# Two-layer decoder trunk: low parts of attention projection weights by accumulating transfers, top-k rounds spread between weight units

## The chip, the core and the metric

The kernel runs on one core of a Trainium2 chip. The metric is device time in microseconds (us) of one execution, the median of the runs shown. The engines are named as in the profile: PE (TensorE, matrix multiply), PEld (its weight loads), DVE (VectorE), ACT (ScalarE), POOL (GpSimd) and SP (SyncE, which here only issues transfers).

## What is computed

One sequence of 512 tokens, width 1024, two layers. Layer 0 is a gated recurrent block, layer 1 is attention over a chosen subset of keys; each is followed by a squared-ReLU MLP of width 4096. Everything is float32. The part that the change touches is the attention layer:

```python
def dsa_mixer(h, w_in, kv_norm_g, w_uk, w_uv, w_o, rel_bias):
    topk = min(TOPK_MAX, S // 4)                            # 128 of 512 keys
    q, c, qi, ki, wi = jnp.split(h @ w_in, ATT_IN_SPLITS, axis=-1)
    c = rms_norm(c, kv_norm_g)                              # latent keys/values, 128 wide
    q_lat = jnp.einsum('bshd,hdc->bshc', q, w_uk) * ATT_SCALE
    ...
    dots = jax.nn.relu(jnp.einsum('bqhd,bsd->bqhs', qi_b, ki))   # 8 index heads
    score = jnp.einsum('bqh,bqhs->bqs', wi_b, dots)              # causal
    _, idx = lax.top_k(score, topk)                              # per query
    logits = q_lat_b . c_sel + bias;  p = softmax(logits);  o = p . c_sel
    ...
    return o @ w_o
```

## The kernel before

**Three products for one.** Each float32 matrix product is made of three PE passes over rounded operands of type float32r. A weight tile `raw` is split into a high part `wh` (the rounded copy, made by ACT, line 268) and a low part `wl = raw - wh` (line 269); activations are split in the same way into `xh` and `xl`. `mm3` (lines 295 to 297) then runs wh with xh, wh with xl and wl with xh into one PSUM accumulator.

**Weight units.** All weights are cut into units of 128x1024 numbers (512 KB), eight blocks of 128x128 each, in the order in which they are used (`PLAN`, `SEQ`). One unit is 24 matmuls. `unit(u)` hands out a unit and prepares those up to five ahead (`LA = WH - 1`), so that loads (line 223, issued by SP), the cast on ACT and the subtraction on DVE or POOL run ahead of PE. There are six buffers for `wh` and six for `wl`, so the cast of a unit waits until PE is done with the unit six before it. `LO_POOL` names the 16 units whose low part POOL makes: of the indexer projections `a_idx` 0, 1, 2 and 4, all eight of the query projection `a_q`, the value matrix `uv`, and the first three of the output projection `w_o`. All others are made by DVE.

**The attention stage.** After the MLP of layer 0, five `a_idx` units give the index queries and keys; after the second of them the mean square of the tokens is taken (`att_st0`: PE line 377, then a chain of small DVE instructions on 128x4 numbers, lines 385 to 396, called with ACT's square root in `rsqrt_tok` and `diag`), and after the third it is broadcast to all partitions by two matmuls with ones (`bcast`, lines 413 and 414). `idx_head` then forms the scores of eight heads; some (head, row block) pairs are scaled and added by POOL (`SCORE_POOL`, lines 872 and 874), the others by DVE (line 876). One unit `a_c` gives the latent keys. The two `uk` units are split by ACT (line 246) and POOL (`ukl`, line 248).

**Top-k** finds the 128th largest score of each row by rounds of eight: the maxima (line 931) and their replacement (line 936), for two of the three row blocks in each round, all on DVE. `topk_steps` is a generator, and `pump(n)` issues n rounds; so the program text decides where rounds stand between other DVE work. Once a row block is done its mask is written (lines 941 and 942).

**The order.** `ATT_HEAD` is a list of steps written out by hand: `q` is one query unit (ev_q: scale on DVE, line 1018, then casts on ACT and subtractions on POOL, lines 880 to 883), `pN` is N top-k rounds, `M` is the mean of the latent keys (c_mean: the same chain of small DVE instructions as above), `F` its broadcast and the normalized keys (c_fin), `L` loads a bias, `k`, `A`, `v`, `n` are steps of single heads. Then `ATT_LOOP` runs the heads in a software pipeline. The framework places each engine's instructions in an order near that of the text, and each engine runs its own list in order.

Of the kernel before, what the change touches and what calls it, by code (L numbers as in the profile page):

```python
# [12 lines left out]
F32R = mybir.dt.float32r  # L13
BF16 = mybir.dt.bfloat16
AF = mybir.ActivationFunctionType
ALU = mybir.AluOpType
# [22 lines left out]

ATT_HEAD = ("q q M q F p1 p1 q L3 q L1 L2 p1 q p2 p2 L0 p2 p1 k0 k1 p2 p1 p1 q A1 A0 v00 v01 p1 v02 n0 k2 n1 v03 q "
            "p2 p1 p1000")

ATT_LOOP = "KAa0Bk1b2xyzeGnfgm"
V_ITER = 6
# [94 lines left out]
PLAN, SEQ = build_plan()  # L141
# [3 lines left out]
SRC = []  # L145
# [2 lines left out]
    SRC.append([MEM.setdefault(_k, len(MEM)) for _k in _keys])  # L148
NMEM = len(MEM)

LO_POOL = {PLAN[n][0] + i for n, w in (("a_idx", (0, 1, 2, 4)), ("a_q", range(8)), ("uv", (0,)), ("w_o", range(3))) for i in w}


@with_exitstack
def tile_trunk(ctx: ExitStack, tc: tile.TileContext, xT, wu, prm, bias, out):
    nc = tc.nc
# [10 lines left out]
    def bt(dt, name):  # L167
        cnt[0] += 1
        return big.tile([P, S], dt, tag="b", name=f"{name}_{cnt[0]}")
# [36 lines left out]
    prepped = {}  # L206
    state = {"next": 0}

    def lo_engine(u):
        return nc.gpsimd if u in LO_POOL else nc.vector  # L210

    UK0 = PLAN["uk"][0]

    def load_raw(u):
        res = []
        for i, n in enumerate(SRC[u]):
            raw = wraw.tile([P, 1024], F32, tag="raw", name=f"raw_{u}_{i}")
            if u == 0:
                nc.sync.dma_start(raw[:, :S], wu[n][:, :S])
                nc.sync.dma_start(x[0], xT[:, 0])  # L220
                nc.sync.dma_start(raw[:, S:], wu[n][:, S:])
            else:
                nc.sync.dma_start(raw, wu[n])
            res.append(raw)
        return res
# [11 lines left out]
    def prep(u):  # L237
        raws = pre_raw.pop(u) if u in pre_raw else load_raw(u)
        kind = SEQ[u][0]
        raw = raws[0] if raws else tsum.pop("P3")  # L240
        if UK0 <= u < UK0 + 2:
            h = []
            l = []
            for j in range(2):
                hh = bt(F32R, "ukh")
                nc.scalar.copy(hh, raw[:, j * S:(j + 1) * S])
                ll = bt(F32R, "ukl")
                nc.gpsimd.tensor_sub(ll, raw[:, j * S:(j + 1) * S], hh)
                h.append(hh)
                l.append(ll)  # L250
            prepped[u] = (h, l)
            return
        if kind == "#T1":
            raw = tsum["T1"] = raws[1]
            nc.vector.tensor_sub(raw, raw, raws[0])
        elif kind == "#T2":
            nc.vector.tensor_sub(raw, raw, tsum.pop("T1"))
            tsum["T2"] = raw
        elif kind == "#T4":
            nc.vector.tensor_sub(raw, raw, tsum.pop("T2"))  # L260
        elif kind == "#P7":
            tsum["P3"] = raw
            raw = raws[1]
            nc.vector.tensor_sub(raw, raws[0], raw)
        wh = whl.tile([P, 1024], F32R, tag="wh", name=f"wh_{u}")
        wl = whl.tile([P, 1024], F32R, tag="wl", name=f"wl_{u}")
        for c in ((slice(0, S), slice(S, 2 * S)) if u == 0 else (slice(0, 2 * S),)):
            nc.scalar.copy(wh[:, c], raw[:, c])  # L268
            lo_engine(u).tensor_sub(wl[:, c], raw[:, c], wh[:, c])  # L269
        prepped[u] = (wh, wl)  # L270
        if kind[:2] == "#P":
            prepped[u] += split_act(aq.pop((kind, SEQ[u][1][1])), "a")
# [580 lines left out]
    for t in (1, 2, 3):  # L853
        score[t] = bt(F32, "score")
        w = (t + 1) * P
# [102 lines left out]
    def pump(n):  # L958
        for _ in range(n):
            next(tk, None)  # L960
# [41 lines left out]
    pump(2)  # L1002
    for m, ps in Phase("a_c", nx2.xh, nx2.xl).step():
        ev_c(ps)
    pump(4)
    ukh = []
    ukl = []
    for g in range(2):
# [189 lines left out]

    for w in ATT_HEAD.split():
        if w[0] == "p":  # L1200
# [208 lines left out]
```

## Time and profile before

| | before |
|---|---|
| median of 3 runs | 1099.59 us (1098.83 to 1101.01) |
| the profiled execution, its own time | 1101.33 us |
| its span (first to last instruction) | 1099.5 us |
| busy: PE / DVE / ACT / POOL | 1072.0 / 763.9 / 619.5 / 166.2 us |
| share of the span: PE / DVE / ACT / POOL | 97% / 69% / 56% / 15% |
| granted TensorE clock, mean | 0.98 |
| chain that ended last: PE / DVE / ACT / POOL | 84% / 8% / 5% / 1% |

PE has work nearly all the time, so a change can shorten the run where PE stands idle or runs at a lower granted clock. In the page's 40 slices PE is below nine tenths only in three around the middle (the attention stage, from about 520 to 630 us) and in the last one. The shares are averages over the whole run: what an engine does in the attention stage is read from windows and timelines of that stage.

### The profile page before, as it was taken

What the parts mean: (1) busy time and instruction counts of PE and PEld (TensorE: products, weight loads), DVE (VectorE), ACT (ScalarE), POOL (GpSimd) and SP (SyncE); (2) the same over time, 40 slices, a digit from 0 to 9 for tenths busy, and PEclk for the clock granted to TensorE, in tenths of its full rate; (3) what the DMA queues carried; (4) which work ended last, traced back from release to release, by engine and by line L of the source; (5) the groups of instructions that cost most, each with busy time, mean ns of one, the idle gap of its engine ahead of it and who ended that gap; (6) DMA issues with size and microseconds to landing.
All of it is one profiled execution on the core that took longest, in us unless ns stands there. A gap on an engine that the chain in (4) does not pass through costs nothing.

```text
span 1099.5 us, 13547 instructions
## 1 busy us (share of the span) xinstructions
PE 1072.0 (97%) x4908; PEld 884.2 (80%) x4908; DVE 763.9 (69%) x1175; ACT 619.5 (56%) x1041; POOL 166.2 (15%) x203
## 2 busy tenths in 40 slices
PE   9999999999999999999798899999999999999996
PEld 7887888888888888888686688888888888888885
DVE  6579995555555559987799979845545555557995
ACT  7379754444444546756444789733644444546463
POOL 0000021000000000019387665312000000000000
PEclk9799999999999999999898899999999999999998
DMA  8222233444443445563313212023234444444562
GB/s 308 77 96 77 80 131 115 134 134 136 135 149 129 141 153 172 192 194 123 105 57 115 87 39 69 1 76 117 96 119 150 146 141 153 134 151 137 169 215 77
DMA packets 40532, 138.30 MB, mean 126 GB/s; under 512 B 4625, under 2 KB 4625, under 8 KB 40465
## 3 DMA queue, kind: packets, MB, share of 16 engines
q1 hardware_dynamic: 40032, 136.86, 38.0%
q8 instruction: 38, 0.62, 0.2%
q10 hardware_dynamic: 432, 0.58, 0.2%
q14 instruction: 30, 0.24, 0.1%
HBM read 135.32 MB, written 2.10 MB: 125 GB/s over the span
## 4 chain that ended last, share of the span: by engine, by line
PE 84%; DVE 8%; ACT 5%; issue 1%; POOL 1%; DMA 0%; DVEq 0%; ACTq 0%; POOLq 0%
PE mm L295 16%; PE mm L296 16%; PE mm L297 15%; PE sp L756 9%; PE sp L754 9%; PE sp L755 9%; PE o L1171 2%; DVE work L936 2%; DVE m L931 2%; PE tr L1146 1%; PE st L618 1%; PE qk L1099 1%; ACT wh L268 1%; PE qk L1100 1%; PE qk L1102 1%
## 5 line engine op out<-in xcount | busy, mean ns | idle before, releaser
L268 ACT CAST wh<-raw 128x1024 fp32r<-128x1024 f32 (+1 forms) x228 | 237.8, 1050 | 359.4 <-PE mm L296 206.0
L269 DVE TENSOR_TENSOR wl<-raw,wh 128x1024 fp32r<-128x1024 f32 (+1 forms) x212 | 259.1, 1226 | 210.7 <-ACT wh L268 210.1
L295 PE MATMUL mm<-xh,wh 128*128 128x512 f32 x752 | 295.8, 394 | 0.2 <-ACT xh L355 0.2
L296 PE MATMUL mm<-xl,wh 128*128 128x512 f32 x752 | 295.6, 393 | 0.0
L297 PE MATMUL mm<-xh,wl 128*128 128x512 f32 x752 | 295.3, 393 | 0.0
L296 PEld LDWEIGHTS mm<-xl,wh 128*128 128x128 f32 x752 | 142.8, 190 | 31.0 <-DVE xl L357 1.1
L295 PEld LDWEIGHTS mm<-xh,wh 128*128 128x128 f32 x752 | 143.1, 190 | 30.5 <-ACT xh L355 0.8
L297 PEld LDWEIGHTS mm<-xh,wl 128*128 128x128 f32 x752 | 142.7, 190 | 29.8
L754 PE MATMUL sp<-wh,ah 128*128 128x512 f32 x320 | 124.9, 391 | 0.0
L756 PE MATMUL sp<-wh,al 128*128 128x512 f32 x320 | 124.6, 389 | 0.0
L755 PE MATMUL sp<-wl,ah 128*128 128x512 f32 x320 | 124.5, 389 | 0.0
L269 POOL TENSOR_TENSOR wl<-raw,wh 128x1024 fp32r<-128x1024 f32 x16 | 39.6, 2478 | 332.5 <-ACT wh L268 325.9
L754 PEld LDWEIGHTS sp<-wh,ah 128*128 128x128 f32 x320 | 60.1, 188 | 12.7 <-ACT t L717 0.5
L756 PEld LDWEIGHTS sp<-wh,al 128*128 128x128 f32 x320 | 60.1, 188 | 12.6
L755 PEld LDWEIGHTS sp<-wl,ah 128*128 128x128 f32 x320 | 60.1, 188 | 12.3
L368 POOL TENSOR_TENSOR sq<-sq,sq 128x512 f32<-128x512 f32 x21 | 34.4, 1637 | 210.9 <-ACT sq L364 185.9
L234 DVE TENSOR_TENSOR al<-h,ah 128x512 fp32r<-128x512 f32 x80 | 55.4, 701 | 2.0 <-ACT ah L232 1.7
L754 PE MATMUL sp<-wh,sh 128*128 128x512 f32 x128 | 50.0, 391 | 0.0
L756 PE MATMUL sp<-wh,sl 128*128 128x512 f32 x128 | 49.9, 392 | 0.0
L755 PE MATMUL sp<-wl,sh 128*128 128x512 f32 x128 | 49.8, 389 | 0.0
L719 ACT ACTIVATE h<-t 128x256 f32<-128x256 f32 x128 | 46.5, 411 | 2.1
L232 ACT CAST ah<-h 128x512 fp32r<-128x512 f32 x80 | 46.7, 619 | 0.5
(258 smaller groups left out, 1645.8 us busy)
## 6 DMA issues: line engine op xcount, KB each, us to landing
raw<-in_wu_dram SPq DMA_DIRECT2D x244, 512.0 KB, 3.4
bias<-in_bias_dram SPq DMA_DIRECT2D x16, 256.0 KB, 3.0
x<-in_xT_dram SPq DMA_DIRECT2D x8, 256.0 KB, 6.4
out_dram<-out SPq DMA_DIRECT2D x6, 256.0 KB, 2.1
raw<-in_wu_dram SPq DMA_DIRECT2D x2, 256.0 KB, 3.7
gB<-in_prm_dram SPq DMA_DIRECT2D x2, 256.0 KB, 5.5
out_dram<-out ACTq DMA_DIRECT2D x2, 256.0 KB, 2.9
prm_sb<-in_prm_dram ACTq DMA_DIRECT2D x1, 52.5 KB, 3.5
```

The source lines that it names most:

```text
L232: nc.scalar.copy(h, src)
L234: nc.vector.tensor_sub(l, src, h)
L268: nc.scalar.copy(wh[:, c], raw[:, c])
L269: lo_engine(u).tensor_sub(wl[:, c], raw[:, c], wh[:, c])
L295: nc.tensor.matmul(ps, lhsT=wh, rhs=xh, start=first, stop=False)
L296: nc.tensor.matmul(ps, lhsT=wh, rhs=xl, start=False, stop=False)
L297: nc.tensor.matmul(ps, lhsT=wl, rhs=xh, start=False, stop=last)
L368: nc.gpsimd.tensor_add(self.acc, self.acc, sq)
L719: nc.scalar.square(hq[r][half][:, p * HS:(p + 1) * HS], t[:, half * HS:(half + 1) * HS])
L754: nc.tensor.matmul(ps, lhsT=ah[:, c], rhs=wh[:, n], start=first, stop=False)
L755: nc.tensor.matmul(ps, lhsT=ah[:, c], rhs=wl[:, n], start=False, stop=False)
L756: nc.tensor.matmul(ps, lhsT=al[:, c], rhs=wh[:, n], start=False, stop=last)
```

## The change

The set `LO_POOL` (16 units, low part on POOL) becomes `LO_DMA` (15 units). For a unit in it, ACT first writes `-raw`, rounded to float32r, into `wl`; then POOL issues a transfer that reads the same weights again from DRAM and adds them to `wl`, which leaves `raw - round(raw)`. `wh` is cast as before. In the set are all five `a_idx` units, `a_c`, the eight `a_q` and `uv`; the three `w_o` units of `LO_POOL` go to DVE, and `a_idx` 3 and `a_c`, which were DVE's, join the set. In `ATT_HEAD`, `M` moves up by one query unit and three top-k rounds stand behind it; the four rounds that were pumped ahead of the `uk` units become one.

```diff
-ATT_HEAD = ("q q M q F p1 p1 q L3 q L1 L2 p1 q p2 p2 L0 p2 p1 k0 k1 p2 p1 p1 q A1 A0 v00 v01 p1 v02 n0 k2 n1 v03 q "
-            "p2 p1 p1000")
+ATT_HEAD = ("q M p3 q q F p1 p1 q L3 q L1 L2 p1 q p2 p2 L0 p2 p1 k0 k1 p2 p1 p1 q A1 A0 v00 v"
+            "01 p1 v02 n0 k2 n1 v03 q p2 p1 p1000")
...
-LO_POOL = {PLAN[n][0] + i for n, w in (("a_idx", (0, 1, 2, 4)), ("a_q", range(8)), ("uv", (0,)), ("w_o", range(3))) for i in w}
+LO_DMA = {PLAN[n][0] + i for n, w in (("a_idx", range(5)), ("a_c", (0,)), ("a_q", range(8)), ("uv", (0,))) for i in w}
...
-    def lo_engine(u):
-        return nc.gpsimd if u in LO_POOL else nc.vector
...
         for c in ((slice(0, S), slice(S, 2 * S)) if u == 0 else (slice(0, 2 * S),)):
+            if u in LO_DMA:
+                nc.scalar.mul(wl[:, c], raw[:, c], -1.0)
+                nc.gpsimd.dma_start(wl[:, c], wu[SRC[u][0]][:, c].bitcast(F32R), accum_op=ALU.add)
             nc.scalar.copy(wh[:, c], raw[:, c])
-            lo_engine(u).tensor_sub(wl[:, c], raw[:, c], wh[:, c])
+            if u not in LO_DMA:
+                nc.vector.tensor_sub(wl[:, c], raw[:, c], wh[:, c])
...
-    pump(4)
+    pump(1)
```

How this moves instructions, at three places. In the fences a row is an instruction of the built program: its line, operation, and tiles written and read.

POOL, from the last unit prepared ahead of the indexer's broadcast to the fourth `ukl`. Before (`wl_4383`, `wl_4501`, `wl_4630` are the low parts of the query units 0, 1 and 2):

```order
L269 TENSOR_TENSOR wl_4383<-raw_0_4334,wh_4382 128x1024
L857 AFFINE_SELECT score_4221<-score_4221 128x128
L248 TENSOR_TENSOR ukl_4263<-raw_0_4233,ukh_4261 128x512
L248 TENSOR_TENSOR ukl_4267<-raw_0_4233,ukh_4265 128x512
L269 TENSOR_TENSOR wl_4501<-raw_0_4386,wh_4500 128x1024
L248 TENSOR_TENSOR ukl_4328<-raw_0_4269,ukh_4326 128x512
L269 TENSOR_TENSOR wl_4630<-raw_0_4504,wh_4629 128x1024
L248 TENSOR_TENSOR ukl_4332<-raw_0_4269,ukh_4330 128x512
```

Now (line numbers are those of the changed file; the same three units are `wl_4389`, `wl_4508` and `wl_4638`):

```order
L269 DMA wl_4389<-in_wu_dram 128x1024
L860 AFFINE_SELECT score_4226<-score_4226 128x128
L247 TENSOR_TENSOR ukl_4269<-raw_0_4239,ukh_4267 128x512
L247 TENSOR_TENSOR ukl_4273<-raw_0_4239,ukh_4271 128x512
L269 DMA wl_4508<-in_wu_dram 128x1024
L247 TENSOR_TENSOR ukl_4334<-raw_0_4275,ukh_4332 128x512
L247 TENSOR_TENSOR ukl_4338<-raw_0_4275,ukh_4336 128x512
L269 DMA wl_4638<-in_wu_dram 128x1024
```

Three subtractions became issues of transfers, and the last two `ukl` stand together.

ACT at the same place, from the casts of the first index query to the copy of the broadcast (`rB`). Before:

```order
L880 CAST qia_4295<-mm_4248 64x512
L881 CAST qib_4296<-mm_4248 64x512
L383 ACT_TABLE_LOAD
L383 ACTIVATE sq_4308<-me_4306 128x4
L246 CAST ukh_4326<-raw_0_4269 128x512
L268 CAST wh_4629<-raw_0_4504 128x1024
L246 CAST ukh_4330<-raw_0_4269 128x512
L880 CAST qia_4361<-mm_4336 64x512
L881 CAST qib_4362<-mm_4336 64x512
L416 COPY rB_544_4370<-bc_4367 128x512
```

Now:

```order
L883 CAST qia_4301<-mm_4254 64x512
L884 CAST qib_4302<-mm_4254 64x512
L386 ACT_TABLE_LOAD
L386 ACTIVATE sq_4314<-me_4312 128x4
L268 ACTIVATE wl_4508<-raw_0_4393 128x1024
L245 CAST ukh_4332<-raw_0_4275 128x512
L270 CAST wh_4637<-raw_0_4512 128x1024
L245 CAST ukh_4336<-raw_0_4275 128x512
L268 ACTIVATE wl_4638<-raw_0_4512 128x1024
L883 CAST qia_4367<-mm_4342 64x512
L884 CAST qib_4368<-mm_4342 64x512
L419 COPY rB_544_4376<-bc_4373 128x512
```

Two more instructions of 128x1024 stand behind the square root and ahead of the copy `rB`.

DVE at the end of top-k, where the last two masks are made (line 941) and the last query unit is scaled (line 1018). Before (`wl_5373` and `wl_5379` are units 3 and 4 of `w_o`):

```order
L941 TENSOR_TENSOR work_4620<-work_4620,score_4221 128x512
L269 TENSOR_TENSOR wl_5373<-raw_0_5370,wh_5372 128x1024
L1073 TENSOR_TENSOR kl_5189<-k_5183,kh_5187 128x512
L269 TENSOR_TENSOR wl_5379<-raw_0_5376,wh_5378 128x1024
L1018 TENSOR_TENSOR qf_5229<-mm_5204,rB_545_4372 128x512
L1115 ISA pa_5270,stat_5268<-qk_5269,bias_4954 128x128
```

Now (`wl_5370` and `wl_5376` are units 0 and 1 of `w_o`):

```order
L944 TENSOR_TENSOR work_4628<-work_4628,score_4226 128x512
L1076 TENSOR_TENSOR kl_5204<-k_5198,kh_5202 128x512
L272 TENSOR_TENSOR wl_5370<-raw_0_4891,wh_5369 128x1024
L1021 TENSOR_TENSOR qf_5244<-mm_5219,rB_545_4378 128x512
L272 TENSOR_TENSOR wl_5376<-raw_0_5373,wh_5375 128x1024
L1118 ISA pa_5285,stat_5283<-qk_5284,bias_4969 128x128
```

One subtraction of 128x1024 less stands ahead of the last `qf`; the low parts of units 2, 3 and 4 of `w_o` follow some twenty DVE instructions later, just ahead of another head's `pa`.

## Rows read from the trace of the kernel before

**Rows 1.** Windows: us, busy us (instructions) of PE, PEld, DVE, ACT, POOL; clock, DMA.

```profile
524.30:530.80 6.50, 0.19 (x1) 0.01 (x1) 6.40 (x7) 2.73 (x4) 5.76 (x4) 0.71 0.57 196
530.80:540.00 9.20, 9.18 (x26) 6.99 (x27) 4.11 (x6) 3.04 (x5) 0.00 (x0) 0.64 0.24 81
...
578.40:583.70 5.30, 0.05 (x2) 0.03 (x1) 5.30 (x23) 2.20 (x8) 2.52 (x2) 0.81 0.24 86
...
621.50:633.00 11.50, 8.85 (x33) 6.19 (x32) 8.38 (x26) 8.80 (x24) 7.34 (x10) 0.70 0.50 160
633.00:703.00 70.00, 69.84 (x448) 59.13 (x448) 59.93 (x187) 62.32 (x170) 38.87 (x92) 1.00 0.14 43
703.00:1050.00 347.00, 347.00 (x1582) 288.48 (x1582) 207.19 (x238) 169.06 (x265) 14.75 (x17) 1.00 0.40 129
```

**Rows 2.** Timeline of PE, in brackets idle time before and its releaser.

```profile
530.82 0.76 PE L413 MATMUL bc<-dg,ones_r 128*128 128x512 f32 x1 [6.33 <-DVE dl L396]
...
544.91 0.40 PE L295 MATMUL mm<-xh,wh 128*128 128x512 f32 x1
...
583.68 0.80 PE L413 MATMUL bc<-dg,ones_r 128*128 128x512 f32 x1 [5.25 <-ACT dg L403]
...
626.96 0.91 PE L1099 MATMUL qk<-kh,qb 128*128 128x256 f32 x2 [2.65 <-ACT kh L1071]
```

**Rows 3.** Timeline of DVE, the chain of small instructions ahead of the first broadcast.

```profile
521.84 1.17 DVE L387 TENSOR_TENSOR t<-y 128x4 f32<-128x4 f32 x1
523.04 2.29 DVE L388 SCALAR_TENSOR_TENSOR t<-t,me 128x4 f32<-128x4 f32 x1
525.37 1.19 DVE L389 SCALAR_TENSOR_TENSOR y<-t,y 128x4 f32<-128x4 f32 x1
526.60 2.27 DVE L841 COPY rq<-y 128x4 f32<-128x4 f32 x1
```

**Rows 4.** Timeline of POOL, first weight unit of the stage, then beside that chain.

```profile
490.91 2.41 POOL L269 TENSOR_TENSOR wl<-raw,wh 128x1024 fp32r<-128x1024 f32 x1 [311.07 <-ACT wh L268]
...
520.42 2.56 POOL L248 TENSOR_TENSOR ukl<-raw,ukh 128x512 fp32r<-128x512 f32 x2
522.92 2.39 POOL L269 TENSOR_TENSOR wl<-raw,wh 128x1024 fp32r<-128x1024 f32 x1
525.26 1.28 POOL L248 TENSOR_TENSOR ukl<-raw,ukh 128x512 fp32r<-128x512 f32 x1
526.49 2.35 POOL L269 TENSOR_TENSOR wl<-raw,wh 128x1024 fp32r<-128x1024 f32 x1
528.79 1.27 POOL L248 TENSOR_TENSOR ukl<-raw,ukh 128x512 fp32r<-128x512 f32 x1
```

**Rows 5.** Timeline of DVE, same small instructions later, with POOL idle.

```profile
581.50 0.15 DVE L389 SCALAR_TENSOR_TENSOR y<-t,y 128x4 f32<-128x4 f32 x1
```

**Rows 6.** Timeline of DVE, start of top-k, its one wait, the last query unit.

```profile
561.18 0.42 DVE L931 MAX8 m<-score 128x8 f32<-128x256 f32 x1
...
592.15 0.69 DVE L1018 TENSOR_TENSOR qf<-mm,rB 128x512 f32<-128x512 f32 x1 [1.79 <-PE mm L297]
...
624.33 0.68 DVE L1018 TENSOR_TENSOR qf<-mm,rB 128x512 f32<-128x512 f32 x1
```

**Rows 7.** Waits between 505 and 705 us: total, times, longest.

```profile
DVE score L876 <- POOL score L874: 1.2, 1, 1.2
```

**Rows 8.** Costliest groups of the page: busy, mean ns of one; idle before.

```profile
L268 ACT CAST wh<-raw 128x1024 fp32r<-128x1024 f32 (+1 forms) x228 | 237.8, 1050 | 359.4 <-PE mm L296 206.0
L269 DVE TENSOR_TENSOR wl<-raw,wh 128x1024 fp32r<-128x1024 f32 (+1 forms) x212 | 259.1, 1226 | 210.7 <-ACT wh L268 210.1
...
L269 POOL TENSOR_TENSOR wl<-raw,wh 128x1024 fp32r<-128x1024 f32 x16 | 39.6, 2478 | 332.5 <-ACT wh L268 325.9
```

**Rows 9.** Transfers of weights: landing on the page, issue durations (min/median/max ns).

```profile
raw<-in_wu_dram SPq DMA_DIRECT2D x244, 512.0 KB, 3.4
...
L223 SPq DMA_DIRECT2D raw<-in_wu_dram x244: 327/328/920, 2.6 to 1064.7; - x122
```

## Prediction

> **What bounds the kernel now.** I read the page first (busy shares, the 40 slices), then the waits of PE between 505 and 710 us, then windows cut at those waits, then the timelines of DVE, POOL, ACT and PE around them. Outside the attention stage PE has no hole until the run's last stretch: 347.0 of 347 us after 703 us, and 69.84 of 70 between 633 and 703 [rows 1]. So only what moves the point where PE runs full again, at about 633 us, moves the end, and one for one.
>
> Ahead of that point PE waits three times: 6.33 us before the broadcast of the indexer's norm, 5.25 us before the broadcast of the latent norm, 2.65 us for the cast of a key head [rows 2]. After each the granted clock is low for a while: the 9.2 us behind the first wait read 0.64, which is mostly the lower of the two levels (1.2 and 2.4 GHz), where the engine had been idle before [rows 1].
>
> The first wait has a cause in the trace that is not arithmetic. PE waits for a chain of DVE instructions on 128x4 numbers. Four of them take 1.17, 2.29, 1.19 and 2.27 us [rows 3], while the same kind takes 0.15 us where POOL is idle [rows 5]. Beside each slow one stands a POOL subtraction, and they end together: POOL's at 522.98, 525.31, 526.54 and 528.84, DVE's at 523.01, 525.33, 526.56 and 528.87 [rows 3, 4]. So on this path DVE gets one tiny instruction done per POOL instruction. Two of those subtractions (2.39 and 2.35 us, line 269) are weight low parts that the change takes off POOL; the `ukl` stay.
>
> From 561.2 us on, DVE is the bound: top-k runs from 561.18 to about 621.5 us (the last `qf`, at 624.33, less the two subtractions of 1.23 us and one of 0.6 that the order shows between) with one idle piece, 1.79 us, in which it waits for a query unit from PE [rows 6, 8]. That unit was late because of PE's second wait. The second wait costs the end no more than this 1.79 us, since PE must then wait for the masks in any case.
>
> **The change part by part.** All sums are against the profiled execution (1101.33 us; span 1099.5, so 1.8 us lie around it), which is 1.74 us above the median of 1099.59; I carry the difference over to the median.
>
> *First wait.* In the order of POOL the subtraction ahead of the first two `ukl` becomes an issue, so those two can end before the chain starts at 521.8. The next issue needs ACT's new multiplication behind the square root, some 1.05 us [rows 8] after it, near 522.5; by then the chain, at 0.15 us an instruction, is almost at its two 128x512 products. One `ukl` (1.28 us) may still meet the second product. So the chain ends near 524.3, where PE finishes its unit anyway. PE gets back its hole, 6.5 us, and the slow stretch: 26 matmuls in 9.2 us, where the later stretch does 1582 in 347, or 0.22 us each, 5.7 us for 26; so 3.5 us [rows 1]. Together 10.0. I leave 0.5 for the `ukl` (ends 0 and 1.3) and 0.7 for ACT, which has one extra 128x1024 multiplication ahead of the casts and of the copy of the broadcast (ends 0 and 1.05). Term: -8.8 us.
>
> *Price of an issue on POOL.* No row of before shows one. Below: an issue on SP, 0.33 us [rows 9]. Above: the subtraction that it replaces, 2.48 us [rows 8]. I take 1 us, nearer to the issue. POOL has no work that PE waits for except the scores, so this counts only as a blocker of DVE (rival B). The Trainium skill (SBUF — State Buffer, "Who interferes with whom") says that a DVE instruction with two SBUF inputs contends with a GpSimd instruction that reads SBUF, not with one that only writes it, and that a DVE copy or cast in a two-port mode contends with both. Rows 3 and 4 agree with the first half; no run here shows an issue beside DVE. By the rule the two-input instructions go past an issue, and the term stays; if an issue blocked like a subtraction, it would be rival B's.
>
> *Start of top-k.* The subtraction in front of POOL's share of the scores goes, and DVE's wait for that share is 1.2 us [rows 7]. Ends 0 and 1.2; I take 0.8. Term: -0.8.
>
> *Inside top-k.* The mean of the latent keys now starts one query unit earlier and its small instructions stand between earlier rounds, so ACT and DVE finish it while PE still has two units to do; PE's second wait goes, the query unit is in time, and DVE's idle 1.79 goes. Number and sizes of the rounds are unchanged. Term: -1.8 (ends 0 and 1.8).
>
> *End of top-k.* One 128x1024 subtraction (1.23 us [rows 8]) less stands ahead of the last `qf`, which starts the casts that PE's third wait is for. Ends 0 and 1.2; I take 0.6. Term: -0.6. PE now reaches this point earlier relative to DVE, so it waits longer for the masks and starts again at the low clock. The window there already reads 0.70 [rows 1], so most of that is paid before: 0 to 1.5, I take +0.7.
>
> *Three low parts of `w_o` on DVE.* 3 x 1.23 = 3.7 us, just behind the masks, where DVE has 3.1 us idle in 11.5 [rows 1]. They delay the next head's reductions by what DVE has not idle there; behind them POOL, ACT and PE wait, but PE has matmuls of other heads queued. Ends 0 and 2.5; I take +1.0.
>
> *ACT.* 15 more instructions of 1.05 us, 15.8 us in all. Six stand in the end of the MLP and nine in the attention stage, where ACT is busy less than half of the time in the three windows around the waits [rows 1]; each stands beside the cast of its own unit or of a neighbour and waits for a buffer that this cast waited for. Beyond the 0.7 above I cost them at nothing; the cover is ACT's idle time, and without it each costs up to 1.05. The low part of `a_idx` 3 and `a_c` leaves DVE (2.5 us at the end of the MLP), where PE is full: nothing.
>
> *The transfers.* Each reads 512 KB again. A plain load lands in 3.4 us [rows 9]; an adding one must also read and write its target, so an estimate is two to three times that, 7 to 10 us. The units are prepared five ahead, each worth 24 matmuls; and the first is asked for at about 491, some 39 us ahead of the first broadcast [rows 2, 4]. Only a queue of them could be late (rival A). The Trainium skill (DMA: Bandwidth & Descriptors, "Anatomy of one DMA") gives a GpSimd-issued transfer 2.0 us plus its bytes at 436 GB/s; by it, as an estimate, one would take 3.2 us and none would be late. No run here shows one.
>
> Sum: -8.8 - 0.8 - 1.8 - 0.6 + 0.7 + 1.0 = -10.3 us, so **1089.3 us** for the median. With every term at its good end -10.0 - 1.2 - 1.8 - 1.2 = -14.2, or 1085.4; at its bad end -10.0 + 1.3 + 1.05 + 1.5 + 2.5 = -3.7, or 1095.9.
>
> **The rivals.**
>
> A, slower: the adding transfers are served one after another and slowly. The five `a_idx` units are asked for within some 15 us from 491; at T us each the fifth is there at 491 + 5T. Before, PE starts that unit at 544.91 [rows 2]. With T = 10.8 that is reached and the first wait's gain is gone; the later terms (about 2 us) remain, so the run gets slower from T of about 11.2. At T = 12.5 the unit comes at 553.5, 8.6 us late, and the sum is +8.6 - 1.8, or 1106.4. For it: three times a plain load is near that bound, and loads share the same 16 engines. Against it: these are 0.24 to 0.57 busy around there [rows 1], so transfers need not go one by one. 0.12.
>
> B, half the gain: an issue holds DVE up as a subtraction did. The issue near 522.5 would end at 525.0, the `ukl` behind it at 526.3, and the two products come between and after them, near 527.5. The hole shrinks by 3.3 us only, and part of the slow clock stays (2 of 3.5 us). The sum is -10.3 + 3.2 + 2 = -5.1, or 1094.5. For it: rows 3 and 4 show DVE held for whole POOL instructions of two forms. Against it: an issue need not read the tile. 0.14.
>
> C, no change: the first hole closes, but what releases top-k is then ACT with its extra instructions (each 1.05 us; nine in the stage make 9.5 us), so top-k starts when it did. Near 1099, within 0.2%. For it: ACT's list is in order and several of the new instructions wait for buffers. Against it: its busy share there is about a half. 0.06.
>
> **How the numbers follow.** Forecast 0.68, A 0.12, B 0.14, C 0.06. A measurement of this kernel can tell about 0.2% (2.2 us) from no change. Faster: 0.68 + 0.14 = 0.82; same 0.06; slower 0.12. The range for 8 in 10 takes in the forecast's own ends and B, and leaves out A and C: 1084.5 to 1096.5; the ends lie 1 us outside the sums for terms that no row shows.
>
> **What would show it.** Right: the DVE chain in front of line 413's first matmul takes 0.15 us an instruction; PE's first wait is under 2 us; top-k's first maximum starts near 551.5 instead of 561.18 and its last mask near 609.5; PE's second wait is gone; its wait before the masks is longer than 2.65 us; POOL's busy time falls by about 39 us and ACT's rises by 16. Wrong: PE waiting at lines 295 to 297 for a transfer into `wl` (A); small DVE instructions still over 1 us beside an issue on POOL (B); top-k starting after 555 us with PE or DVE waiting for ACT (C). If the chain is short and the span is not, a step behind the masks, the three `w_o` low parts first of all, is the one that failed.

## Result, and the profile after

| | before | after |
|---|---|---|
| median of 4 runs each | 1099.21 us (1096.08 to 1101.01) | 1090.40 us (1089.42 to 1090.72) |
| the profiled execution / its span | 1101.33 / 1099.5 us | 1090.72 / 1088.9 us |

The ratio is 0.9927, with a 95% interval of 0.9910 to 0.9943. By the medians it is 8.8 us faster (by the ratio 8.0, interval 6.3 to 9.9), where 10.3 were forecast (1089.3 us).

The page of the changed kernel: busy time of the engines, one group (busy us, mean ns, idle before) and two DMA issues (KB each, median us from issue to landing):

```profile
PE 1067.4 (98%) x4908; PEld 880.3 (81%) x4908; DVE 754.4 (69%) x1176; ACT 632.6 (58%) x1056; POOL 140.7 (13%) x202
...
L269 POOL DMA_DIRECT2D wl<-in_wu_dram x15 | 13.2, 879 | 334.4 <-ACT wl L268 326.2
...
raw<-in_wu_dram SPq DMA_DIRECT2D x244, 512.0 KB, 3.4
wl<-in_wu_dram POOLq DMA_DIRECT2D x15, 512.0 KB, 8.0
```

An issue takes POOL 0.88 us, and a transfer lands after 8.0 us (median) where a plain load of the same size lands after 3.4. Nothing waits for one: no row of PE's waits between 500 and 710 us names a transfer. But there is little to spare. Here are the time to landing of the first five transfers, and a window of before and of now (the last two numbers are the busy share of the DMA engines and GB/s):

```profile
DMA to landing us min/median/max: 7.3/8.0/10.7
```

```profile
488.00:520.00 32.00, 31.65 (x158) 26.03 (x157) 25.01 (x29) 20.25 (x29) 26.58 (x17) 1.00 0.44 139
```

```profile
488.00:520.00 32.00, 32.00 (x159) 26.35 (x158) 18.75 (x28) 27.70 (x39) 20.39 (x22) 1.00 1.02 263
```

Each of the five lands later after its issue than the one ahead of it, and the 16 DMA engines are busy all the time from 488 to 520 us, where their share was 0.44.

The two timelines that answer to [rows 3] and [rows 4], DVE's small chain and POOL beside it (start, us, engine, line, operation, tiles; in brackets the idle time ahead and what ended it):

```profile
517.09 0.16 DVE L424 TENSOR_SCALAR me<-st 128x4 f32<-128x4 f32 x1 [4.38 <-PE st L380]
...
520.00 0.16 DVE L390 TENSOR_TENSOR t<-y 128x4 f32<-128x4 f32 x1
...
520.67 0.16 DVE L397 CAST yh<-y 128x4 fp32r<-128x4 f32 x1
520.74 0.68 DVE L409 TENSOR_TENSOR dg<-ident,y 128x512 fp32r<-128x512 f32 x1
521.34 1.89 DVE L399 TENSOR_TENSOR dl<-y,yh 128x4 f32<-128x4 f32 x1
523.26 0.69 DVE L409 TENSOR_TENSOR dg<-ident,dl 128x512 fp32r<-128x512 f32 x1
```

```profile
515.81 2.79 POOL L247 TENSOR_TENSOR ukl<-raw,ukh 128x512 fp32r<-128x512 f32 x2
521.00 0.88 POOL L269 DMA_DIRECT2D wl<-in_wu_dram  x1 [2.40 <-ACT wl L268]
521.62 1.58 POOL L247 TENSOR_TENSOR ukl<-raw,ukh 128x512 fp32r<-128x512 f32 x1
```

The chain runs at 0.16 us an instruction, until `dl` meets the third `ukl`: `dl` takes 1.89 us and ends at 523.23, `ukl` at 523.20. The issue that POOL makes from 521.00 to 521.88 holds nothing up: the `dg` beside it takes its 0.68 us. (`dl` starts beside the issue, too, and 0.28 us ahead of the `ukl`; e7, below, has the same issue and no `ukl` there, and its `dl` takes 0.15 us.)

PE's waits in the stage, answering to [rows 2], and two windows around the last of them (sum of the stretch, busy time of PE, PEld, DVE, ACT and POOL, granted clock, DMA share, GB/s):

```profile
524.01 0.50 PE L417 MATMUL bc<-dg,ones_r 128*128 128x512 f32 x1 [1.12 <-DVE dg L409]
...
594.01 0.38 PE L1102 MATMUL qk<-kh,qb 128*128 128x256 f32 x1 [1.94 <-ACT kh L1074]
...
607.83 0.56 PE L1102 MATMUL qk<-kh,qa 128*128 128x256 f32 x2 [1.87 <-ACT kh L1074]
...
613.55 0.90 PE L1102 MATMUL qk<-kh,qb 128*128 128x256 f32 x2 [0.96 <-ACT kh L1074]
...
623.34 0.35 PE L1102 MATMUL qk<-kh,qb 128*128 128x256 f32 x1 [1.77 <-DVE stat L1118]
```

```profile
530.00:540.00 10.00, 9.68 (x51) 8.46 (x51) 8.96 (x19) 7.91 (x17) 0.86 (x1) 1.00 0.78 172
...
605.00:615.00 10.00, 6.46 (x24) 4.05 (x23) 10.00 (x22) 7.71 (x17) 4.61 (x4) 0.76 0.30 93
615.00:630.00 15.00, 13.07 (x66) 10.23 (x65) 14.07 (x45) 11.75 (x36) 11.86 (x22) 0.82 0.53 183
```

The first wait is 1.12 us in place of 6.33, and the slow clock behind it is gone (1.00 from 530 to 540, where [rows 1] read 0.64). The second wait is gone. The waits for key heads (ACT's `kh`) are now three, of 1.94, 1.87 and 0.96 us, and a new wait stands at 623.34, on DVE.

**Five stretches.** In every kernel of this study the program up to the attention stage is the same, yet the stage starts between 485.4 and 489.5 us. That is settled in the first 60 us, where the granted clock differs from one execution to the next, whatever the kernel. First the kernel before, then one of the experiments below (e6), with the granted clock third from the end:

```profile
0.00:60.00 60.00, 58.58 (x251) 47.27 (x252) 38.10 (x73) 31.74 (x45) 1.00 (x9) 0.89 0.50 177
```

```profile
0.00:60.00 60.00, 58.15 (x266) 46.94 (x267) 39.25 (x73) 34.47 (x48) 0.99 (x9) 0.94 0.55 192
```

At 0.94 the stage starts at 485.40 us, at 0.89 at 488.74. From ACT's eleventh cast of a weight unit, at 38.4 to 42.5 us, to the stage's start all thirteen profiles take 446.9 to 447.0 us. So I compare profiles by stretches of the stage: from its start (ACT's first `xh`) to the chain's end (end of its last `dg`), to the first maximum, to where PE resumes behind the masks (the `qk` matmul of [rows 2]'s last row), to the first `o` matmul, to the end. All in us, each from one profiled execution:

| kernel | start at | to chain's end | to first max | to PE resumes | to first `o` | to the end |
|---|---|---|---|---|---|---|
| before | 488.74 | 42.73 | 29.71 | 65.78 | 11.82 | 460.72 |
| after | 487.32 | 36.63 | 26.45 | 63.15 | 14.71 | 460.64 |
| difference | -1.42 | -6.10 | -3.26 | -2.63 | +2.89 | -0.08 |

Of the 10.6 us between the two profiled executions 9.2 lie behind the start and 1.4 ahead of it. The profiled execution of the kernel before (1101.33 us) is at the slow end of that kernel's runs (1095.34 to 1101.34 us on the three chips below), so its stretches may be on the long side; e3 will show where.

### The profile page after: what moved, and what is told of

Read it like the earlier page. It is cut to its first block, busy times and chain, and to the rows that moved or that the text cites. A ratio compares the mean times of both kernels' runs of the same rounds, so it can differ in the third digit from the quotient of the medians.

```text
span 1088.9 us, 13588 instructions
## 1 busy us (share of the span) xinstructions
PE 1067.4 (98%) x4908; PEld 880.3 (81%) x4908; DVE 754.4 (69%) x1176; ACT 632.6 (58%) x1056; POOL 140.7 (13%) x202
## 4 chain that ended last, share of the span: by engine, by line
PE 87%; DVE 7%; ACT 3%; issue 2%; POOL 1%; DMA 1%; SPq 0%; DVEq 0%; POOLq 0%; ACTq 0%
PE mm L298 16%; PE mm L299 16%; PE mm L300 16%; PE sp L757 9%; PE sp L759 9%; PE sp L758 9%; PE o L1174 3%; DVE work L939 2%; DVE m L934 2%; PE tr L1149 1%; PE st L621 1%; PE qk L1103 1%; PE qk L1102 1%; PE qk L1105 1%; DMA raw<-in_wu_dram 1%
## 5 line engine op out<-in xcount | busy, mean ns | idle before, releaser
L269 POOL DMA_DIRECT2D wl<-in_wu_dram x15 | 13.2, 879 | 334.4 <-ACT wl L268 326.2
```

## The experiments

Each run is compared with the kernel before on the same chip, in three groups (1098.09, 1096.85 and 1097.22 us before), so between groups the ratios and the stretches count, not the bare times. Ratios have their 95% interval in brackets. Line numbers shift by a few lines from kernel to kernel.

| run | median us | ratio | chain's end | first max | resumes | first `o` |
|---|---|---|---|---|---|---|
| e1 `w_o` back on POOL | 1085.45 | 0.9883 (0.9867, 0.9899) | 36.64 | 26.46 | 63.58 | 9.68 |
| e2 transfers alone | 1090.87 | 0.9924 (0.9907, 0.9941) | 36.63 | 26.47 | 65.29 | 11.54 |
| e3 order alone | 1094.99 | 0.9969 (0.9956, 0.9982) | 42.70 | 28.19 | 64.05 | 9.46 |
| e4 three units | 1091.41 | 0.9931 (0.9915, 0.9947) | 37.07 | 27.35 | 66.48 | 10.54 |
| e5 POOL, two inputs | 1092.48 | 0.9962 (0.9949, 0.9974) | 37.92 | 27.84 | 63.57 | 12.53 |
| e6 POOL, no input | 1090.48 | 0.9939 (0.9923, 0.9955) | 34.92 | 28.20 | 63.14 | 14.69 |
| e7 e1 and `ukl` transfers | 1083.82 | 0.9880 (0.9866, 0.9895) | 34.91 | 26.71 | 63.15 | 10.66 |
| e8 e2 and `w_o` on POOL | 1087.65 | 0.9917 (0.9902, 0.9932) | 36.63 | 26.47 | 66.65 | 9.69 |
| e9 `w_o` by transfers | 1087.02 | 0.9901 (0.9884, 0.9918) | 36.64 | 26.45 | 64.30 | 9.67 |
| e10 three units, new order | 1087.81 | 0.9914 (0.9902, 0.9927) | 37.04 | 27.33 | 64.05 | 9.46 |
| e11 three units on DVE, new order | 1087.48 | 0.9911 (0.9897, 0.9925) | 37.27 | 27.01 | 64.07 | 9.45 |

**e1: the three `w_o` low parts back on POOL.**

```diff
+LO_POOL = {PLAN[n][0] + i for n, w in (("w_o", range(3)),) for i in w}
...
             if u not in LO_DMA:
-                nc.vector.tensor_sub(wl[:, c], raw[:, c], wh[:, c])
+                (nc.gpsimd if u in LO_POOL else nc.vector).tensor_sub(wl[:, c], raw[:, c], wh[:, c])
```

> The changed kernel with one part undone: the first three low parts of the output projection go back to GpSimd, the 15 transfers and the new order of the top-k rounds stay. Theory: in the changed kernel three subtractions on VectorE (1.43 + 2.36 + 2.36 us from 618.85) stand ahead of the last pa of the first heads, PE then waits 1.77 us and runs slow until about 627.5, and that is where 2.9 us of the gain were given back. Without them 2 to 3 us come back: 1087.5 to 1088.5 us. Rival: the give-back belongs to the end of the top-k masks (ScalarE's kh, the last mask), and VectorE's subtractions only fill a wait that would be there anyway; or GpSimd's subtractions, 2.4 us each, hold VectorE just as long: 1090 to 1091 us.

Measured 1085.45 us: more than the theory's 2 to 3 us came back. First DVE in the changed kernel, then PE in this one:

```profile
618.85 1.43 DVE L272 TENSOR_TENSOR wl<-raw,wh 128x1024 fp32r<-128x1024 f32 x1
...
620.27 2.36 DVE L272 TENSOR_TENSOR wl<-raw,wh 128x1024 fp32r<-128x1024 f32 x2
622.56 0.28 DVE L1118 CUSTOM_DVE_ANT_0 pa<-qk,bias 128x128 f32<-128x128 f32 x1
```

```profile
620.56 0.29 PE L1104 MATMUL qk<-kh,qb 128*128 128x256 f32 x1
...
623.38 0.48 PE L1176 MATMUL o<-pth,vh 128*128 128x512 f32 x1
```

In the changed kernel the reductions (`pa`, `stat`) of the next head start behind three subtractions, 3.7 us in all (the row with x2 gives the time of both together, which the expectation counted twice). By the order of the built program these are units 2, 3 and 4 of `w_o`; units 0 and 1 stand at 609.78 and 611.52, where e1 has units 3 and 4. So three units more on DVE put three subtractions behind the masks. PE's `qk` at 623.34 waits for them. In e1 the same `qk` (620.56) follows without a hole, and from resuming to the first `o` it is 9.68 us instead of 14.71. Of these 5.0 us not all are the subtractions' own. e5, below, keeps them on DVE and has the full clock there:

```profile
590.00:605.00 15.00, 12.47 (x47) 9.90 (x46) 15.00 (x43) 8.07 (x11) 7.61 (x9) 0.78 0.01 2
605.00:615.00 10.00, 9.29 (x42) 7.32 (x41) 9.66 (x25) 8.24 (x21) 3.81 (x6) 0.98 0.00 0
615.00:630.00 15.00, 10.94 (x61) 7.46 (x61) 14.96 (x41) 11.04 (x32) 13.29 (x18) 1.00 0.65 214
```

It takes 12.53 us, so 2.9 us are theirs at the full clock. The other 2.2 us go with the slow clock (0.76 and 0.82 in the changed kernel's windows above). There it falls twice, as one and the same form of matmul shows:

```profile
614.66 0.88 PE L1102 MATMUL qk<-kh,qb 128*128 128x512 f32 x1
...
619.18 0.48 PE L1102 MATMUL qk<-kh,qa 128*128 128x512 f32 x1
...
626.44 0.88 PE L1102 MATMUL qk<-kh,qb 128*128 128x512 f32 x1
```

The first slow stretch costs 0.6 us against e5, since PE then waits for DVE anyway (9.79 against 9.22 us from resuming to the `qk` that waits). The second stands right behind that wait and costs 1.6 us (4.92 against 3.31 us from this `qk` to the first `o`). e6 has both stretches, too. In e5, which waits 2.19 us for DVE, and in e1 (0.77), the slow stretch fell at 590 to 605, ahead of the masks, where PE has to wait in any case. Why it falls here or there is open, and so is whether the subtractions bring on the second one.

**e2 and e3: the two halves of the change alone.** e2 has the new low parts and the old order; e3 the old low parts and the new order. The edit of e2 against the changed kernel (e3 makes the opposite edit to the kernel before):

```diff
-ATT_HEAD = ("q M p3 q q F p1 ...
+ATT_HEAD = ("q q M q F p1 ...
...
-    pump(1)
+    pump(4)
```

> The 15 transfers (and the output projection's low parts on VectorE), with the order of the top-k rounds of the kernel before. Theory: the first wait goes with the subtractions beside VectorE's small chain, so 8 to 9.5 us of the gain are here: 1090 to 1092 us, with 0 to 1.8 us left to the order. Rival (the order does it, since VectorE gets its top-k rounds without a gap): 1095 to 1099 us.

> The kernel before with the new order of the top-k rounds alone; all 16 low parts stay on GpSimd. Theory: the small chain on VectorE still runs beside GpSimd's subtractions, so PE still waits some 6 us for it: 1097.5 to 1100 us. Rival (the order does it): 1090 to 1094 us. If the order puts rounds in the chain's way it is slower, 1100 to 1103 us.

e2: 1090.87 us, as the theory had it; the first two stretches are those of the changed kernel to 0.02 us. e3 is a miss: 3.4 us of gain by the ratio, where the theory had 2 at the most. Its chain is as slow as before (42.70 against 42.73), as the theory said. But the new order takes 1.7 us from the stretch to where PE resumes. Two other stretches are shorter as well, by 1.5 us before the first maximum and by 2.4 us behind the resumption. There it is the clock. The first of the two, before and in e3:

```profile
531.47:561.18 29.71, 29.04 (x127) 24.02 (x127) 21.11 (x32) 16.89 (x36) 11.71 (x11) 0.90 0.16 53
```

```profile
529.68:557.87 28.19, 27.53 (x127) 22.94 (x127) 21.11 (x31) 16.88 (x36) 11.71 (x11) 0.95 0.16 57
```

The engines do the same work behind the same wait of PE (6.33 and 6.32 us), and the granted clock is 0.90 and 0.95. Behind the resumption it is 0.75 before and 1.00 in e3. That the order does this is not shown: the three stretches add up to 5.6 us, the runs to 3.4. By the ratios the halves are worth 8.3 and 3.4 us alone, 11.7 in sum, and 8.0 together: something in the changed kernel takes 3.7 us back, give or take 3 (the three intervals taken together, an estimate).

**e8: the fourth corner of the square.**

It is e2 with e1's edit:

```diff
+LO_POOL = {PLAN[n][0] + i for n, w in (("w_o", range(3)),) for i in w}
```

> The 15 transfers, the order of the top-k rounds of the kernel before, and the output projection's first three low parts on GpSimd. It completes the square of order (old, new) and place of those parts (VectorE, GpSimd): old and VectorE 1090.87, new and VectorE 1090.40, new and GpSimd 1085.45. Theory: the new order is worth 3 to 5 us, which the subtractions on VectorE take back in the changed kernel since they fall ahead of the last pa there; in the old order they fall into VectorE's time before PE resumes and cost 0 to 1.5 us: 1089 to 1091 us. Rival: the subtractions cost 5 us in either order, and the order is worth nothing: 1085 to 1086.5 us.

1087.65 us lies between the two ranges; the ratio and the stretches decide, for the theory. With `w_o` on POOL the new order is worth 3.7 us (ratio 0.9917 to 0.9883; from the first maximum to the first `o` 76.34 to 73.26 us), with `w_o` on DVE nothing (0.9924 to 0.9927; 76.83 to 77.86 us).

Seen the other way, `w_o` on DVE costs 4.8 us in the new order and 0.8 in the old one (by the stretch 4.6 and 0.5). So what takes the gain back is `w_o` on DVE together with the new order: 4.0 us by the ratios, give or take 3.6 (an estimate, as above), and 4.1 by the stretch. Only part of the 4.1 is explained. In the old order three of the five subtractions stand ahead of the first `pa` behind the masks and two behind it (in e2 from 621.46), in the new one two and three. Behind the resumption, at the full clock, that costs 1.9 us in the old order (11.54 against 9.69) and 2.9 in the new one (e5 against e1), which makes 1.0. Another 2.2 are the slow clock of the changed kernel, which is open, and 0.9 lie ahead of the resumption, where `w_o` on DVE is the faster way in both orders (65.29 against 66.65 us, 63.15 against 63.58).

The order's own gain is DVE's idle time in top-k. The windows of e8 (old order) and then of e1 (new order):

```profile
575.00:590.00 15.00, 15.00 (x63) 12.23 (x62) 12.71 (x38) 8.11 (x12) 12.55 (x10) 0.92 0.56 157
...
605.00:615.00 10.00, 8.20 (x32) 5.92 (x30) 9.12 (x20) 8.09 (x15) 4.60 (x6) 0.83 0.23 72
```

```profile
575.00:590.00 15.00, 15.00 (x68) 12.43 (x67) 15.00 (x45) 6.88 (x10) 13.73 (x11) 1.00 0.58 167
590.00:605.00 15.00, 12.40 (x46) 9.77 (x45) 15.00 (x46) 10.00 (x21) 11.90 (x14) 0.77 0.22 84
605.00:615.00 10.00, 7.62 (x36) 5.41 (x35) 9.66 (x19) 7.32 (x15) 4.09 (x4) 1.00 0.25 85
```

DVE is idle for 2.29 and 0.88 us there in e8 and for 0 and 0.34 in e1, 2.8 us less (the 2.29 are its one wait for a query unit, 1.79 us in [rows 6]); PE resumes 3.1 us sooner after the first maximum (63.58 against 66.65).

**e4: only the three units beside the chain.**

Old order, and (against the kernel before, with the changed kernel's lines that use `LO_DMA`)

```diff
+LO_DMA = {PLAN[n][0] + i for n, w in (("a_q", range(3)),) for i in w}
-LO_POOL = {PLAN[n][0] + i for n, w in (("a_idx", (0, 1, 2, 4)), ("a_q", range(8)), ...
+LO_POOL = {PLAN[n][0] + i for n, w in (("a_idx", (0, 1, 2, 4)), ("a_q", range(3, 8)), ...
```

> The kernel before, old order, with the low parts of only the first three query units formed by accumulating transfers (the three subtractions that GpSimd ran at 517.83, 522.92 and 526.49, beside VectorE's small chain); the other 13 stay on GpSimd. Theory: what counts is what GpSimd does beside that chain, so these three bring most of the gain: minus 7 to 9 us, 1090 to 1092.5 us. Rival (GpSimd has to be lighter over the whole stage, or the transfers keep VectorE and ScalarE supplied): 3 of 16 of the gain, about 1097 us.

1091.41 us, ratio 0.9931: nearly all that e2 gains with 15 transfers (0.9924). e8 (0.9917) is the fairer comparison, since it has `w_o` on POOL as e4 does: from the stage's start to the first `o` e4 takes 141.44 us, e8 139.44 and the kernel before 150.04, so the three units bring 8.6 of 10.6 us. The chain's stretch is 37.07 against 36.63.

**e5 and e6: is it that POOL reads, or that POOL is busy?** Both add useless work of POOL to the changed kernel at those three units.

```diff
+    scr = [cpool.tile([P, 192], BF16, name=f"scr{i}") for i in range(3)]
...
+        if 0 <= u - PLAN["a_q"][0] < 3:
+            t = scr[u - PLAN["a_q"][0]]
+            nc.scalar.copy(t[:, :1], wh[:, :1])
+            for _ in range(5):
+                nc.gpsimd.tensor_sub(t, raw[:, :192], wh[:, :192])
```

In e6 the last two lines are `for _ in range(10):` and `nc.gpsimd.memset(t, 0.0)`.

> The changed kernel with extra work on GpSimd that nobody uses: behind the hi part of each of the first three query units five subtractions of 192 columns (two SBUF inputs, into a scratch tile), some 2.5 us for each unit, about where the old subtractions stood; ScalarE writes one column of the scratch tile first (some 0.2 us, three times), so that the work can't start earlier. Theory: it is GpSimd's instructions with two SBUF inputs that hold VectorE, so the small chain (6.86 us from me to the end of the last dg now, 12.55 us before) grows again by 2 to 6 us, and the time to 1092 to 1096 us. Rival (the chain was held by the scheduler's order or by something else that went with the subtractions, such as the wait for ScalarE's hi part): 1090 to 1091 us, chain within 0.5 us of 6.86.

> The same as the kernel with the extra subtractions, but with ten memsets of 192 columns in place of each five subtractions: GpSimd is as long busy (some 2.5 us a unit) and reads nothing. Theory: chain within 0.5 us of 6.86 us, 1090 to 1091.5 us. Rival (what counts is that GpSimd is busy, so that what follows it, the ukl parts and the scores, comes later): as slow as the one with the subtractions, 1092 to 1096 us.

DVE's chain and then POOL beside it, in e5 and then in e6:

```profile
521.38 0.44 DVE L396 TENSOR_TENSOR t<-y 128x4 f32<-128x4 f32 x1
521.86 0.16 DVE L397 SCALAR_TENSOR_TENSOR t<-t,me 128x4 f32<-128x4 f32 x1
522.05 0.45 DVE L398 SCALAR_TENSOR_TENSOR y<-t,y 128x4 f32<-128x4 f32 x1
...
522.62 0.58 DVE L403 CAST yh<-y 128x4 fp32r<-128x4 f32 x1
...
523.71 2.15 DVE L405 TENSOR_TENSOR dl<-y,yh 128x4 f32<-128x4 f32 x1
```

```profile
520.27 2.89 POOL L278 TENSOR_TENSOR scr<-raw,wh 128x192 bf16<-128x192 f32 x4
...
523.73 1.56 POOL L248 TENSOR_TENSOR ukl<-raw,ukh 128x512 fp32r<-128x512 f32 x1
```

```profile
518.10 0.16 DVE L396 TENSOR_TENSOR t<-y 128x4 f32<-128x4 f32 x1
...
518.77 0.20 DVE L403 CAST yh<-y 128x4 fp32r<-128x4 f32 x1
...
519.44 0.16 DVE L405 TENSOR_TENSOR dl<-y,yh 128x4 f32<-128x4 f32 x1
```

```profile
516.82 3.07 POOL L278 MEMSET scr<- 128x192 bf16 x9
```

Beside subtractions of 0.72 us (2.89 for four) three of the small instructions take 0.44, 0.45 and 0.58 us. (`dl` meets a `ukl` and a subtraction behind it.) Beside nine memsets, 3.07 us without a gap, they take 0.16 to 0.20 (one copy 0.27, where it takes 0.17 in the changed kernel). Chains of 8.09 and 5.09 us (from `me` to the last `dg`; 6.86 in the changed kernel), and 1092.48 against 1090.48 us. So it is POOL's subtractions that hold DVE, not a busy POOL. (A POOL instruction that reads a single input was not tried.) The times lie in the theory's ranges, the chains do not: in e5 it grew by 1.2 us, where 2 to 6 were expected, since shorter POOL instructions hold DVE for less each; in e6 it is 1.8 us shorter, where at most 0.5 was expected, since the memsets pushed the third `ukl` past the chain. There 1.75 us were given back before the first maximum (28.20 against 26.45), where PE now waits 1.66 us for ACT's `kiwi`.

**e7: the four `ukl` by transfers too** (with `w_o` on POOL as in e1).

```diff
-                nc.gpsimd.tensor_sub(ll, raw[:, j * S:(j + 1) * S], hh)
+                nc.scalar.mul(ll, raw[:, j * S:(j + 1) * S], -1.0)
+                nc.gpsimd.dma_start(ll, wu[SRC[u][0]][:, j * S:(j + 1) * S].bitcast(F32R), accum_op=ALU.add)
```

> The changed kernel with the output projection's first three low parts back on GpSimd and, new, the four ukl parts (128x512) formed by accumulating transfers as well. Theory: the one ukl subtraction left beside the small chain holds its dl for 1.89 us in place of 0.15, so 1.2 to 1.7 us go: 1083.7 to 1084.5 us against 1085.45. Rival: ScalarE's four further multiplications (0.6 us each) and GpSimd's issues (0.9 us each) come in the same 10 us, and qia, rB and kiwi on ScalarE come later by as much: 1085 to 1087 us.

POOL and then DVE:

```profile
520.99 0.87 POOL L272 DMA_DIRECT2D wl<-in_wu_dram  x1 [3.16 <-ACT wl L271]
```

```profile
521.33 0.15 DVE L402 TENSOR_TENSOR dl<-y,yh 128x4 f32<-128x4 f32 x1
```

`dl` takes 0.15 us beside an issue (520.99 to 521.86), and the chain is 1.73 us shorter than in e1. The time is 1083.82 us, the lowest of the study and 1.2% below the kernel before; the stretches from start to end sum to 595.70 us against e1's 596.68. But by the ratios (0.9880 and 0.9883) the two can't be told apart.

**e9: `w_o` off DVE in another way.**

```diff
-... ("uv", (0,))) for i in w}
+... ("uv", (0,)), ("w_o", range(3))) for i in w}
```

> The changed kernel with the output projection's first three low parts formed by accumulating transfers too (18 transfers; ScalarE multiplies by minus one three times more, 1.05 us each). Theory: what the changed kernel lost at the end of the top-k masks is VectorE's time for these three, so it comes back whichever way they leave VectorE: 1085 to 1086.5 us, and the stretch from the first max to the first o matmul, 77.86 us now and 73.26 us with them on GpSimd, is 73 to 74 us. Rival: what came back with them on GpSimd was a luckier place of TensorE's slow stretch, or ScalarE's further 3 us delay kh and the masks there: 1088 to 1090.5 us, 75 to 78 us.

The median, 1087.02 us, lies between the two ranges and its runs are spread (1084.79 to 1089.02). The stretch decides for the theory: 73.97 us from the first maximum to the first `o`, 9.67 of it behind the resumption. So by the stretch it doesn't matter where the three go, if they leave DVE; the ratio alone (0.9901, interval to 0.9918) could not tell e9 from the changed kernel (0.9927, from 0.9910).

**e10 and e11: are the transfers needed at all?** Both have the new order, POOL as before for 13 units, and the first three query units by transfers (e10) or by DVE (e11). The line in which the two differ:

```diff
-LO_DMA = {PLAN["a_q"][0] + i for i in range(3)}    # e10
+LO_DMA = set()                                     # e11
```

> The kernel before with the new order of the top-k rounds and only the first three query units by transfers; the other 13 low parts stay on GpSimd. Theory, with the three stretches of the earlier runs added up (stage start to the end of the chain 37.07 as with the three units alone, to the first max 27.35 or less, to the first o matmul 73.3 to 73.5 as with the order alone): 1.0 to 1.5 us behind the kernel with 15 transfers and the output projection's parts on GpSimd (136.36 in sum), 1086 to 1087.5 us. Rival (the other twelve transfers are needed in the top-k stage, since GpSimd's subtractions there hold VectorE's rounds): 1089 us or more.

> The kernel before with the new order of the top-k rounds, no transfers at all, and the low parts of the first three query units on VectorE (1.2 us each) instead of GpSimd; the other 13 stay on GpSimd. Theory: the second of these subtractions stands in VectorE's row ahead of the small chain and waits there for ScalarE's hi part, which comes at about 522.5, so the chain waits behind it although nothing holds VectorE any more: stage start to chain end 39 to 43 us (36.63 with transfers, 42.73 before), 1090 to 1095 us. Rival: taking the subtractions off GpSimd is all that is needed, and 1.2 us each on VectorE are cheap: 37 to 38.5 us, 1086 to 1088 us.

e10: 1087.81 us, a little over the range; from the stage's start to the first `o` 137.88 us against e1's 136.36, 1.5 us behind, as added up. e11 is a miss, and the rival holds: 1087.48 us with no transfer at all. DVE:

```profile
517.91 0.16 DVE L426 TENSOR_SCALAR me<-st 128x4 f32<-128x4 f32 x1 [2.29 <-PE st L382]
...
518.20 1.98 DVE L274 TENSOR_TENSOR wl<-raw,wh 128x1024 fp32r<-128x1024 f32 x1
...
521.85 0.76 DVE L392 TENSOR_TENSOR t<-y 128x4 f32<-128x4 f32 x1
```

The subtraction ahead of the chain (518.20) did not have to wait for ACT: its unit's cast had ended at 517.65, and the one at 522.5, which the expectation named, is the next unit's. It takes 1.98 us beside a `ukl`, mostly in a time in which the chain waits for the square root: from `me` to the first link it is 3.72 us (517.91 to `y` at 521.63) where the changed kernel takes 2.70. That costs the first part of the chain 1.0 us. In all the chain is no longer than in the changed kernel, 6.76 against 6.86 us, since the third `ukl` is past before `dl`, which takes 0.16 us; its end comes 0.6 us later (37.27 against 36.63) since `me` starts later.

## Why the prediction was right, and where it was not

**First wait and start of top-k: right in size and cause.** Predicted -8.8 - 0.8 = -9.6; the first two stretches give -9.36 (of it 1.5 us may be the one execution of the kernel before: e3, behind the same wait, has that much less of the slow clock). That the cause is POOL's subtractions beside the chain is shown by e4, e11 and the pair e5 and e6; that the clock behind the wait belongs to it, by the windows. The `ukl` term of 0.5 (ends 0 and 1.3) was a little small: the chain without it is 1.7 us shorter (e7). ACT's extra multiplications (0.7) show at most in PE's wait of 0.33 us for ACT's `kiwi` at 530.34, which the kernels without them (before, e3, e11) do not have. By how much they delay is not measured.

**Price of an issue: right.** 0.88 us measured, 1 us taken, and it holds up no DVE instruction beside it (`dg` in the changed kernel, `dl` in e7), so rival B is out. Rival A is out, since PE waits for no transfer, but not for the reason given. The median of 8.0 us to landing is in the 7 to 10 of the estimate. Yet the first five do queue, behind each other or behind the loads, at DMA engines that are full (1.02) and not 0.24 to 0.57 busy as in the rows of before: they land 4.0 us apart on the mean, where the rival needed 10.8, and the fifth is there at 513 us. Rival C is out: the first maximum came at 550.40, forecast 551.5, with PE's longest wait ahead of it at 1.12 us.

**Inside and end of top-k: right in size.** Predicted -1.8 - 0.6 = -2.4; PE resumes 2.63 us sooner after the first maximum. e3 (-1.7), the pair e8 and e1 (-3.1) and the pair e2 and the changed kernel (-2.1) show that the order does this. DVE's idle 1.79 us in top-k is gone, as forecast.

**The `w_o` low parts: the step that failed.** Predicted +1.0 with an end of 2.5; the stretch from resuming to the first `o`, in which the +0.7 for the slow clock was to be found too, grew by 2.89. The slow clock cost some 2.2 us there before as well (11.82 us against 9.5 to 9.7 at full clock), and costs as much now, so in this pair its difference is about nothing and the 2.9 are what the subtractions cost at full clock in e5. But that the sum came so near is in part luck. e1 is the change without these subtractions, and its stretch is 2.1 us shorter than before, where the forecast for the slow clock was +0.7; against e1 the subtractions, with the second slow stretch behind them, cost 5.0 and not 1.0. Two misses of opposite sign left 1.2 us. The step's mistake: "PE has matmuls of other heads queued". PE runs one list in order, and the next thing in it was the `qk` whose accumulator that reduction frees. Their own time was as predicted, 3.7 us; what failed is that DVE's idle time (3.1 us in the window of [rows 1], 2.7 from resuming to the first `o`) would take most of it: it fell by 1.8 us, to 0.9, and the rest came on top.

**What stands beside the forecast.** 10.3 us were forecast and 8.8 came by the medians. Of the difference 1.2 us are the `w_o` term (2.9 against 1.0 + 0.7); the rest is within the scatter of the start. The last stretch, from the first `o` to the end, is as long as before (-0.08 us), so what moves the first `o` moves the end one for one, as forecast. One sign did not come as told: PE's wait before the masks is not one wait longer than 2.65 us but three of at most 1.94, 4.8 us in all where the two of before make 3.4. POOL's busy time fell by 25.5 us and not by 39, since the page counts the issues as busy (13.2 us); ACT's rose by 13.1.

## What to carry to other kernels

A chain of tiny instructions is held by a neighbour for the length of the neighbour's instructions; so find the few that stand beside the chain and move these: three units brought 8.6 of the 10.6 us of fifteen transfers, and as much without a transfer. Two edits that each gain can cancel in part: look where a moved piece of work lands after the other edit has moved the idle time. And compare profiles by stretches between landmarks, since the clock at a program's start can shift all of it by 4 us; a stretch, too, is worth what its granted clock is, so read that beside it.

## What was not expected of the hardware

- The granted clock of the first 60 us differs from execution to execution, 0.89 to 0.94, and shifts everything behind by up to 4 us (485.4 to 489.5).
- An accumulating transfer of 512 KB lands after 8.0 us (5.3 to 11.7, median of 15), a plain one after 3.4; the Trainium skill (DMA: Bandwidth & Descriptors, "Anatomy of one DMA") would by its figures have it at 3.2 us, an estimate, and the measurement decides.
- POOL's memsets do not hold DVE's small instructions of two inputs (0.16 us beside nine of them), its subtractions do (0.44 to 2.29). This agrees with the Trainium skill (SBUF — State Buffer, "Who interferes with whom"): a DVE instruction with two SBUF inputs contends with a GpSimd instruction that reads SBUF, not with one that only writes it. Copies and casts of one input were held by the subtractions as well (2.27 us in [rows 3], 0.58 in e5), and hardly by the memsets (0.27 and 0.20). That an issue of a transfer does not hold instructions of two inputs either is shown here for two of them (`dg` of 0.68 us beside 0.88, `dl` of 0.15 beside 0.87).
- Behind one and the same wait of PE, 6.3 us, the granted clock of the next stretch read 0.90 before and 0.95 in e3, which is 1.5 us of 29.71.
